# A fourth buffer for the out-state weights beside the output projection, their lag products placed one set later, and one buffer for the normed rows

## The chip, the cores and the metric

One Trainium2 chip (trn2), of which the kernel uses one core. The metric is the device time of one execution in microseconds (us), the median of several runs; lower is better. The engines are TensorE (PE), VectorE (DVE), ScalarE (ACT), GpSimd (POOL) and SyncE (SP, which here only starts transfers).

## The reference

Two layers share one residual stream of D = 1024 features. Layer 0 is windowed attention with grouped heads, layer 1 a bidirectional S5 state space with a gated linear unit. There are 512 latent tokens and 256 context tokens; the branch is 2048 wide.

```python
for i in range(DEPTH):                      # DEPTH = 2: attention, then S5
    h = x * (1.0 + scale) + shift           # the same for the context xc
    pz = h @ w_in                           # branch input and gate path z
    y, yc = attention_mixer(...) or s5_mixer(...)
    x = layer_norm(alpha * x + gate * ((y * silu(z)) @ w_out[i]))
    xc = layer_norm(alpha * xc + gate_c * ((yc * silu(zc)) @ w_out[i]))   # not in the last layer
```

The S5 mixer needs, for each of 128 groups, matrices built from the powers of its complex poles: "out-state" weights, with which a chunk's incoming state acts on its outputs, and lag kernels, with which the inputs act on the outputs of the same chunk. They depend on parameters alone, so the kernel builds them beside layer 0.

## The kernel before

The 768 tokens are six blocks of 128: 0 to 3 latent, 4 and 5 context. Every fp32 product is three products of split operands (`mm3`, L155 to L157): high times high, high times low, low times high. A high part is a copy on ACT, a low part a subtraction on DVE (for the gated heads L145 and L146, for the output weights L582 and L583). Tiles live in pools with a number of buffers each; a scheduler, which works with priorities and a model of the engines, fixes the order of each engine's instructions beforehand, and the pools get fixed addresses, in which a later pool may lie over an earlier one.

**Layer 0's stages.** Attention and its projections (pz, pzc) run to about 666 us; the last steps of a head are the scores, their transposes PT, the split `pth`/`ptl`, the product O, and a store of the gated heads to DRAM (gsc). Then comes the output projection, `outproj0`, to about 843 us: it runs in two halves of 512 columns, each with 8 weights (`wr` raw; `wh` and `woh` high, `wl` and `wol` low), in the first half over the blocks [0,1,2], 3, 4, 5 and in the second over [5,4,0], 1, 2, 3. `gsrc` loads four heads of a block at once (a chunk, 256 KB, from ACT's queue) into one of two raw buffers `gr` and splits them into one of five pairs `gh`/`gl`; each chunk feeds 12 products into `po`. `body` then forms R on DVE (L627, L628), and in the second half the normed rows `nrm` (L633), which PE transposes (h1t, L1021), ACT and DVE turn into the next layer's split input (H1H, H1L), and for latent blocks a store keeps (L636). Behind it layer 1 begins with its input projection: `puc` of context blocks, then `pul` of the latent ones.

**Beside it** the out-state weights are made, 32 sets in all, by `gen_o` (L904): POOL multiplies and adds nine times per set (L924 to L926, then per direction L939, L940, L941 into a tile `gO`), from operands `gcb` and `gpp` that SP loads. ACT fills the tile's edge (L937), SP stores it (osc). Its `lag()` runs 8 small products on PE (L956, 16 rows in the profile), which are evicted into `gK` and stored. `out_q` calls the lag of a set after the next set's `gen_o`. Sets 0 to 19 belong to the attention stage, with four gO buffers; sets 20 to 31 to the pool `go2`, opened in the stage of `outproj0` and served by `side()`, with three. Where a pool has more than three, the first lag product is tied to the last POOL instruction of the next set (L957): the tie is for the scheduler alone, and the engine does not wait for it.

Of the kernel before, what the change touches and what calls it, by code (L numbers as in the profile page):

```python
# [111 lines left out]
F32 = mybir.dt.float32  # L112
# [21 lines left out]
class K:  # L134
# [125 lines left out]
    def ada_gate(self, pool, gpool, l, rows, gscale, gtag):  # L260

        nc, a = self.nc, self.a
        gb = pool.tile([128, 1024], F32, name="gb", tag=gtag, bufs=2)
        nc.sync.dma_start(gb, a["adab"][l, 2048:3072].partition_broadcast(128))
        gates = []
        for r in rows:
            g = gpool.tile([128, 1024], F32, name=f"gate{l}{r}", bufs=1)
            for j in range(2):
                nc.sync.dma_start(g[:, j * 512:(j + 1) * 512], self.gm[64 * l + 32 * j + r].partition_broadcast(128))
            nc.vector.tensor_add(g, g, gb)  # L270
            nc.vector.tensor_scalar(g, g, gscale, None, op0=ALU.mult)
            gates.append(g)
        return gates
# [293 lines left out]
def out_half(k, l, half, groups, gsrc, wpool, body, side=lambda: None):  # L567

    nc, a = k.nc, k.a
    cs = slice(half * 512, half * 512 + 512)  # L570
    W = []
    for c in range(8):
        src = a["wout"][l, c * 256:(c + 1) * 256, cs].rearrange("(e p) n -> p e n", p=128)
        raw = k.wp.tile([128, 2, 512], F32, name="wr", tag="wr", bufs=2)
        if c < 2:
            hi = k.wp.tile([128, 2, 512], F32R, name="wh", tag="wh", bufs=2)
            lo = k.wp.tile([128, 2, 512], F32R, name="wl", tag="wl", bufs=2)
        else:
            hi = wpool[0].tile([128, 2, 512], F32R, name="woh", bufs=6)
            lo = wpool[1].tile([128, 2, 512], F32R, name="wol", bufs=6)  # L580
        nc.sync.dma_start(raw, src)
        nc.scalar.activation(hi, raw, AF.Copy)  # L582
        nc.vector.tensor_sub(lo, raw, f32(hi))  # L583
        W.append((hi, lo))
    for bs in groups:

        n = 256 if half == 1 and bs == groups[-1] else 512
        g = [gsrc(bs[0], e) for e in range(16)] if n < 512 else None
        for c0 in range(0, 512, n):
            po = [k.ps.tile([128, 512], F32, name="po", tag="pj")[:, :n] for b in bs]  # L590
            for e4 in range(0, 16, 4):
                for b, o in zip(bs, po):
                    for e in range(e4, e4 + 4):
                        gh, gl = g[e] if g else gsrc(b, e)
                        wh, wl = (w[:, e % 2, c0:c0 + n] for w in W[e // 2])
                        k.mm3(o, gh, gl, wh, wl, e == 0, e == 15)
            for b, o in zip(bs, po):
                body(b, o, slice(half * 512 + c0, half * 512 + c0 + n))
                side()


def outproj0(k, side):
    tc, nc, a = k.tc, k.nc, k.a
    order = [[[0, 1, 2][:NG]] + [[b] for b in range(NG, 6)], [[5, 4, 0], [1], [2], [3]]]
    R = {}
    g = {}

    def gsrc(b, e):
        if e % 4 == 0:
            ts = slice(b * 128, b * 128 + 128)  # L610
            g[1] = (g.get(1, -1) + 1) % 5
            g[0] = k.load_split(k.gop, "g", [128, 4, 128], k.gsc[e // 4][:, :, ts].rearrange("e p t -> p e t"), 2, 1, nc.scalar, g[1])
        return g[0][0][:, e % 4], g[0][1][:, e % 4]

    def body(half):
        def f(b, po, cs):
            ts = slice(b * 128, b * 128 + 128)
            n = cs.stop - cs.start
            if half == 0:
                r = k.rpool.tile([128, 512], F32, name=f"R{b}")  # L620
            else:
                r = k.op.tile([128, 512], F32, name="R2", bufs=2)
            r = r[:, :n]
            R.setdefault(b, []).append((r, cs))
            xt = k.op.tile([128, 512], F32, name="xt", bufs=2)[:, :n]
            nc.sync.dma_start(xt, a["xtok"][ts, cs])
            nc.vector.tensor_mul(r, po, k.gates0[0 if b < 4 else 1][:, cs])  # L627
            nc.vector.scalar_tensor_tensor(r, xt, ALPHA, r, op0=ALU.mult, op1=ALU.add)  # L628
            if cs.stop == 1024:
                n = k.op.tile([128, 1024], F32, name="nrm", bufs=2)  # L630
                mean, rstd = k.norm(R[b], k.np)
                for x, s in R[b]:
                    nc.vector.tensor_scalar(n[:, s], x, mean, rstd, op0=ALU.subtract, op1=ALU.mult)  # L633
                k.make_h1(b, n)
                if b < 4:
                    nc.sync.dma_start(k.n0[ts], n)  # L636
        return f
    for half in range(2):
        out_half(k, 0, half, order[half], gsrc, k.wop, body(half), side)
# [254 lines left out]
def open_o(k, pool, q0, q1, gob):  # L894

    k.gob, k.dq = gob, q0
    k.dd = pool.tile([128, 16 * (q1 - q0)], F32, name="dd")
    k.nc.sync.dma_start(k.dd, k.a["dd"][:, 16 * q0:16 * q1])
    sg = pool.tile([128, 2], F32, name="sg")
    k.nc.sync.dma_start(sg, k.a["sgn"])  # L900
    k.sg = sg[:, 0:1]
# [96 lines left out]
def prep_h1(k):  # L998

    nc, a = k.nc, k.a  # L1000
    shT, scT = k.sh1
    gc, bc = k.ld("lngc0", [128, 8], a["lngc"][0]), k.ld("lnbc0", [128, 8], a["lnbc"][0])
    G = k.cp.tile([128, 2, 8], F32, name="h1g")
    B = k.cp.tile([128, 2, 8], F32, name="h1b")
    for r in range(2):
        nc.vector.tensor_mul(G[:, r], scT[:, r], gc)
        nc.vector.tensor_mul(B[:, r], scT[:, r], bc)
        nc.vector.tensor_add(B[:, r], B[:, r], shT[:, r])
    k.h1g, k.h1b = G, B


def make_h1(k, b, n):
    nc = k.nc
    r = 0 if b < 4 else 1
    ts = slice(b * 128, b * 128 + 128)
    hf = k.op.tile([128, 8, 128], F32, name="h1f", bufs=1)
    for j in range(2):
        t = k.ps.tile([128, 4, 128], F32, name="h1t", tag="T", bufs=2)
        for i in range(4):
            kk = 4 * j + i  # L1020
            nc.tensor.transpose(t[:, i], n[:, kk * 128:(kk + 1) * 128], k.ident)  # L1021
        for i in range(4):
            kk = 4 * j + i
            g, c = k.h1g[:, r, kk:kk + 1], k.h1b[:, r, kk:kk + 1]
            nc.scalar.activation(hf[:, kk], t[:, i], AF.Identity, bias=c, scale=g)
    H, Lo = k.H1[r]
    ts = slice((b - 4 * r) * 128, (b - 4 * r) * 128 + 128)
    nc.scalar.activation(H[:, :, ts], hf, AF.Copy)
    nc.vector.tensor_sub(Lo[:, :, ts], hf, f32(H[:, :, ts]))
# [310 lines left out]
QA, NB = 20, 5  # L1340
# [7 lines left out]
def main(tc, a):  # L1348
    gw = None
    nq = 0  # L1350
    nc = tc.nc
    k = K(tc, a)
# [4 lines left out]
    def opener(es):  # L1357
        def P(name, bufs=1, **kw):
            if kw.get("space") != DRAM:
                kw["reuse_waits"] = "tile"  # L1360
            return es.enter_context(tc.tile_pool(name=name, bufs=bufs, **kw))
        return P
    with contextlib.ExitStack() as es:
# [106 lines left out]
        with contextlib.ExitStack() as e2:  # L1470
            Q = opener(e2)
            wh = Q("woh")
            k.op = Q("op")
            k.gop = Q("gop")
            k.wop = wh, Q("wol")
            k.rpool = Q("rpool")
            k.make_h1 = lambda b, n: make_h1(k, b, n)
            k.gates0 = k.ada_gate(k.op, k.rpool, 0, (0, 1), 0.5, "nrm")
            prep_h1(k)
            e4 = contextlib.ExitStack()  # L1480
            gw = opener(e4)("go2", side="right")
            open_o(k, gw, QA, 32, 3)
            nb = 0

            def side():
                nonlocal nb
                nb += 1
                if nb <= NB:
                    out_q(QA + (QO - QA) * nb // NB, nb == NB)
                    if nb == NB:  # L1490
                        e4.close()
            outproj0(k, side)
            k.uu = opener(h1c)("uu", side="right")
            first = [uproj_ctx(k, blk) for blk in range(2)]
# [3 lines left out]
        with contextlib.ExitStack() as e2:  # L1498
# [3 lines left out]
            with contextlib.ExitStack() as e3:  # L1502
                R = opener(e3)
                S = []
                with contextlib.ExitStack() as e4:
                    k.up = opener(e4)("up", side="right")
                    e6 = contextlib.ExitStack()
                    gw = opener(e6)("go3")
# [86 lines left out]
```

## Time and profile before

| | |
|---|---|
| time, median of 3 runs | 1488.96 us (1484.08 to 1492.28) |
| the profiled execution: its own time, its span | 1486.36 us, 1484.6 us |
| mean granted clock of PE | 0.983 |
| busy: PE, DVE, ACT, POOL | 1389.9, 1016.6, 667.6, 604.8 us |
| PE waits for a set's gO before lag products, 640 to 850 us | 14.1 us in 8 pieces |

Times inside the span are us from its start. In a timeline a row has the start, the busy time, the engine, the line, the operation, output <- input, how often, and in brackets the idle time before it with what ended it; a queue (ACTq, SPq) shows when a transfer is started. In a row of windows the stretch is followed by its length; then for PE, PEld (PE's weight loads), DVE, ACT and POOL the busy us and, in brackets, the number of instructions; then the granted clock of PE as a share of full speed, the busy share of the DMA engines, and GB/s.

### The profile page before, as it was taken

To read this page: it belongs to the slowest core of one execution; us is meant where nothing else is said; L and a number is where in the kernel's file an instruction comes from. 1 tells how busy PE (TensorE), PEld (TensorE's weight loads), DVE (VectorE), ACT (ScalarE), POOL (GpSimd) and SP (SyncE) were. 2 spreads that over 40 slices of the span, in tenths; PEclk is the share of its full clock that TensorE was granted. 3 is DMA by queue.
4 is the path that set the end of the run, shared out by engine and by line. 5 is a ranking of instruction groups with operands and counts; after the bars stand their busy time and mean duration, and the time that the engine had idled before them with its cause. 6 is when DMAs were issued, how large, how long until landed. Compare 5 with 4: busy or idle time off the path is not lost. (4 is left out here: it accounts for less than half of the span.)

```text
span 1484.6 us, 25841 instructions
## 1 busy us (share of the span) xinstructions
PE 1389.9 (94%) x9092; PEld 1123.2 (76%) x9092; DVE 1016.6 (68%) x2751; ACT 667.6 (45%) x1344; POOL 604.8 (41%) x542
## 2 busy tenths in 40 slices
PE   7999999999986999989878899999999999999997
PEld 2554788898875788877766798888777777888876
DVE  7735748777673677875658813798989986574476
ACT  1310546466463657563333634445556545343220
POOL 0004459999998567973999500000000000000240
PEclk9999999999997999999999999999999999999999
DMA  9876566766674446478697576766767786554541
GB/s 336 284 232 204 161 189 205 230 204 213 190 239 157 132 155 207 148 224 270 200 272 233 178 241 216 223 214 216 239 230 241 242 277 216 182 198 156 185 137 61
DMA packets 252930, 309.60 MB, mean 209 GB/s; under 512 B 45568, under 2 KB 151936, under 8 KB 252800
## 3 DMA queue, kind: packets, MB, share of 16 engines
q1 hardware_dynamic: 227456, 295.36, 62.5%
q10 hardware_dynamic: 25344, 12.59, 2.9%
q8 instruction: 72, 1.18, 0.3%
q14 instruction: 58, 0.48, 0.1%
HBM read 239.20 MB, written 77.07 MB: 213 GB/s over the span
## 5 line engine op out<-in xcount | busy, mean ns | idle before, releaser
L1323 POOL TENSOR_TENSOR xt<-xt,lng 128x512 f32<-128x512 f32 (+1 forms) x9 | 13.3, 1480 | 592.7 <-issue 559.0
L146 DVE TENSOR_TENSOR wl<-wr,wh 128x1024 fp32r<-128x1024 f32 x104 | 142.9, 1374 | 137.7 <-ACT wh L145 135.6
L145 ACT ACTIVATE wh<-wr 128x1024 fp32r<-128x1024 f32 x104 | 109.9, 1058 | 192.7 <-PE pul L156 54.2
L155 PE MATMUL pg<-ga,wh 128*128 128x512 f32 x256 | 100.3, 392 | 0.7 <-ACT ga L1248 0.7
L157 PE MATMUL pg<-ga,wl 128*128 128x512 f32 x256 | 100.5, 393 | 0.0
L887 POOL TENSOR_TENSOR gm<-gB,gE 128x512 f32<-128x512 f32 x56 | 77.7, 1387 | 24.2 <-DVE zs L502 19.9
L941 POOL TENSOR_TENSOR gO<-gO,gX 128x512 f32<-128x512 f32 x58 | 85.2, 1469 | 3.9
L489 DVE TENSOR_TENSOR ptl<-PT,pth 128x512 fp32r<-128x512 f32 (+1 forms) x96 | 60.5, 638 | 36.6 <-ACT pth L488 35.9
L888 POOL TENSOR_TENSOR gm<-gB,gE 128x512 f32<-128x512 f32 x56 | 84.2, 1503 | 0.0
L462 ACT ACTIVATE P<-P,nm 128x512 f32<-128x512 f32 (+1 forms) x64 | 49.6, 775 | 67.2 <-DVE nm L445 66.8
L940 POOL TENSOR_TENSOR gX<-gcb,gpp 128x512 f32<-128x512 f32 x58 | 76.5, 1320 | 3.2
L146 DVE TENSOR_TENSOR gl<-gr,gh 128x512 fp32r<-128x512 f32 x48 | 53.3, 1113 | 33.8 <-ACT gh L145 33.7
L939 POOL TENSOR_TENSOR gO<-gcb,gpp 128x512 f32<-128x512 f32 x58 | 71.5, 1242 | 11.4 <-issue 4.1
L1112 DVE TENSOR_TENSOR x<-m 128x64 f32<-128x64 f32 x376 | 74.5, 217 | 2.4
L155 PE MATMUL O<-pth,vh 128*128 128x256 f32 x176 | 53.4, 303 | 20.4 <-ACT zs L499 12.0
L155 PE MATMUL pq<-hh,wh 128*128 128x512 f32 x160 | 65.9, 413 | 2.8 <-ACT hh L255 2.8
L469 ACT ACTIVATE P<-P,es 128x512 f32<-128x512 f32 (+2 forms) x96 | 61.0, 684 | 15.6 <-DVE es L467 15.3
L156 PE MATMUL pq<-hl,wh 128*128 128x512 f32 x160 | 66.1, 413 | 1.2 <-DVE hl L256 1.2
L488 ACT ACTIVATE pth<-PT 128x512 fp32r<-128x512 f32 (+1 forms) x96 | 52.2, 558 | 31.9 <-PE PT L485 24.9
L485 PE MATMUL PT<-ident,P 128*128 128x128 f32 x352 | 61.6, 277 | 4.4 <-DVE vl L388 3.4
L157 PE MATMUL pq<-hh,wl 128*128 128x512 f32 x160 | 65.1, 407 | 0.3 <-DVE wl L146 0.3
L145 ACT ACTIVATE gh<-gr 128x512 fp32r<-128x512 f32 x48 | 30.2, 630 | 71.5 <-DMA gr<-gsc 44.4
(317 smaller groups left out, 4675.5 us busy)
## 6 DMA issues: line engine op xcount, KB each, us to landing
wr<-w SPq DMA_DIRECT2D x40, 512.0 KB
osc<-gO SPq DMA_DIRECT2D x64, 256.0 KB
wr<-wout SPq DMA_DIRECT2D x32, 512.0 KB
W<-wsc SPq DMA_DIRECT2D x32, 512.0 KB
om<-osc SPq DMA_DIRECT2D x64, 256.0 KB
wr<-glu SPq DMA_DIRECT2D x32, 512.0 KB
gE<-esc SPq DMA_DIRECT2D x56, 256.0 KB
gB<-bt SPq DMA_DIRECT2D x56, 256.0 KB
```

Of the source, the lines that this page charges most:

```text
L145: nc.scalar.activation(hi, raw, AF.Copy)
L146: nc.vector.tensor_sub(lo, raw, f32(hi))
L155: mm(out, wh, mh, start=start, stop=False)
L156: mm(out, wh, ml, start=False, stop=False)
L157: mm(out, wl, mh, start=False, stop=stop)
L485: nc.tensor.transpose(T[:, j, h, :], P[h][:, c * 128:(c + 1) * 128], k.ident)
L887: tt(x(m1), x(B), eb(0), op=ALU.mult)
L888: tt(x(m2), x(B), eb(1), op=ALU.mult)
L939: eng.tensor_tensor(o8, cc(0), pb(0), op=ALU.mult)
L940: eng.tensor_tensor(x8, cc(1), pb(36), op=ALU.mult)
L941: last = eng.tensor_tensor(o8, o8, x8, op=ALU.add)
L1112: nc.vector.tensor_add(x, m[:, :, 0], m[:, :, 1])
```

## The change

The pool `go2` gets a fourth gO buffer (2304 bytes on each partition). With four, the tie of L957 applies to it too, so each lag is placed behind the POOL work of the following set. The normed rows get one buffer instead of two, and so does `gb`, a row of the gate's bias that shares their tag (4096 bytes). The sums done are the same.

```diff
@@ ada_gate
-        gb = pool.tile([128, 1024], F32, name="gb", tag=gtag, bufs=2)
+        gb = pool.tile([128, 1024], F32, name="gb", tag=gtag, bufs=1 if gtag == "nrm" else 2)
@@ outproj0, body
-                n = k.op.tile([128, 1024], F32, name="nrm", bufs=2)
+                n = k.op.tile([128, 1024], F32, name="nrm", bufs=1)
@@ the stage around outproj0
             gw = opener(e4)("go2", side="right")
-            open_o(k, gw, QA, 32, 3)
+            open_o(k, gw, QA, 32, 4)
```

The pools move: the one with `gr` by 4096 bytes, so that the buffer of every second load now lies over the low part hl of the last block of attention's input and over the tables of the rotary positions, where it lay over rotary temporaries.

On PE, before, 193 products of `po` stand ahead of the first lag of `go2`'s sets and 35 to 39 between one and the next in the first 400; the lag of the last set stands within the last block's products of `po`:

```order
L155 MATMUL po<-woh,gh 128x256
L156 MATMUL po<-wol,gh 128x256
L956 MATMUL lag<-gO,gbb 32x128 x8
L1021 MATMUL h1t<-ident,nrm 128x128 x8
L157 MATMUL po<-woh,gl 128x256
```

After, 209 stand ahead of the first and 46 between one and the next; the last two sets' lags stand ahead of the next layer's `pul`:

```order
L155 MATMUL puc<-H1H_8278,wh 128x256
L156 MATMUL puc<-H1L_8279,wh 128x256
L157 MATMUL puc<-H1H_8278,wl 128x256
L1021 MATMUL h1t<-ident,nrm 128x128 x8
L956 MATMUL lag<-gO,gbb 32x128 x16
L155 MATMUL pul<-H1H_8273,wh 128x384
```

The last of the small products moved past the rest of `po` and all 48 of `puc`.

On ACT, before, at the end of the attention (the numbers tell tiles of a name apart: gr_8377, gr_8395 and gr_8413 are the first three loads of the output projection, wh_8327, wh_8333 and woh_8339 its first three weights, pth_8232 and pth_8250 the attention's last):

```order
L144 DMA gr_8377<-gsc0_74 128x4x128
L144 DMA gr_8395<-gsc0_74 128x4x128
L582 ACTIVATE wh_8327<-wr_8326 128x1024
...
L145 ACTIVATE gh_8450<-gr_8449 128x512
L582 ACTIVATE wh_8333<-wr_8332 128x1024
L582 ACTIVATE woh_8339<-wr_8338 128x1024
...
L488 ACTIVATE pth_8232<-PT_8227 128x512
L144 DMA gr_8485<-gsc2_76 128x4x128
L488 ACTIVATE pth_8250<-PT_8245 128x512
```

After:

```order
L582 ACTIVATE wh_8333<-wr_8332 128x1024
L582 ACTIVATE woh_8339<-wr_8338 128x1024
L144 DMA gr_8377<-gsc0_74 128x4x128
L937 ACTIVATE gO_7925<-gcb_7916,sg_4709 128x4x16
L144 DMA gr_8395<-gsc0_74 128x4x128
...
L488 ACTIVATE pth_8232<-PT_8227 128x512
L145 ACTIVATE gh_8378<-gr_8377 128x512
L488 ACTIVATE pth_8250<-PT_8245 128x512
```

The first loads fell back behind the third weight, and the first split of a chunk stands between the last two pth.

On SP, before, the operands of `go2`'s first sets stand behind a load of an output weight (dd and sg are small constants of the pool):

```order
L581 DMA wr<-wout 128x2x512 x2
L966 DMA ksc<-gK 128x240
L581 DMA wr<-wout 128x2x512
L898 DMA dd<-dd 128x192
L900 DMA sg<-sgn 128x2
L910 DMA gcb<-cb 128x512 x2
L912 DMA gpp<-ppsc 128x160 x2
```

After:

```order
L966 DMA ksc<-gK 128x240
L581 DMA wr<-wout 128x2x512
L898 DMA dd<-dd 128x192
L900 DMA sg<-sgn 128x2
L910 DMA gcb<-cb 128x512 x2
L912 DMA gpp<-ppsc 128x160 x2
L581 DMA wr<-wout 128x2x512
```

They moved ahead of one weight load.

## Rows read from the trace of the kernel before

**Rows 1.** Which engines are busy, page section 1 (us, share of the span, instructions):
```profile
PE 1389.9 (94%) x9092; PEld 1123.2 (76%) x9092; DVE 1016.6 (68%) x2751; ACT 667.6 (45%) x1344; POOL 604.8 (41%) x542
```

**Rows 2.** Waits of the stretch 640 to 850 us (us in total, times, longest):
```profile
PE lag L956 <- POOL gO L941: 14.1, 8, 3.5
...
PE lag L956 <- POOL gX L925: 1.8, 1, 1.8
```

**Rows 3.** Busy time of each engine by stretch, 710 to 838 us:
```profile
710.00:785.00 75.00, 62.83 (x337) 49.00 (x337) 46.12 (x51) 25.44 (x52) 72.26 (x60) 0.95 0.84 251
...
785.00:838.00 53.00, 44.73 (x305) 35.49 (x303) 50.14 (x104) 27.90 (x69) 50.13 (x44) 1.00 0.62 187
```

**Rows 4.** Timeline of PE, first and last two of six lags before 785 us:
```profile
717.31 0.65 PE L956 MATMUL lag<-gO,gbb 128*32 128x128 f32 x16 [0.99 <-POOL gO L941]
...
764.00 0.65 PE L956 MATMUL lag<-gO,gbb 128*32 128x128 f32 x16 [2.82 <-POOL gO L941]
...
774.88 0.64 PE L956 MATMUL lag<-gO,gbb 128*32 128x128 f32 x16 [1.84 <-POOL gO L941]
```

**Rows 5.** Timeline of DVE, start and end of the last chain of blocks:
```profile
785.80 0.69 DVE L627 TENSOR_TENSOR R<-po,gate 128x512 f32<-128x512 f32 x1 [0.75 <-PE po L157]
...
848.49 1.19 DVE L633 TENSOR_SCALAR nrm<-R,mv,nt 128x512 f32<-128x512 f32 x3
```

**Rows 6.** Timeline of PE, first product of the next layer:
```profile
851.40 0.44 PE L155 MATMUL pul<-H1H,wh 128*128 128x384 f32 x1 [1.16 <-ACT h1f L1025]
```

**Rows 7.** Timeline of PE, first product of the output projection:
```profile
666.82 0.54 PE L155 MATMUL po<-wh,gh 128*128 128x512 f32 x1
```

**Rows 8.** Windows behind two of those waits, granted clock behind the counts:
```profile
764.70:768.00 3.30, 3.30 (x15) 2.73 (x16) 0.56 (x1) 1.58 (x2) 3.07 (x4) 1.00 0.95 298
...
776.00:780.00 4.00, 4.00 (x12) 3.10 (x11) 1.14 (x3) 0.95 (x3) 3.69 (x4) 0.57 1.13 345
```

**Rows 9.** Tile lag in 480 to 640 us: what its 15 sets waited for:
```profile
  POOL gO L941: 0.7, 2
```

**Rows 10.** Timeline of ACT, around the attention's end and after it:
```profile
650.82 0.39 ACTq L144 DMA_DIRECT2D gr<-gsc  x1
...
656.50 0.63 ACT L145 ACTIVATE gh<-gr 128x512 fp32r<-128x512 f32 x1 [1.99 <-DMA gr<-gsc]
...
659.70 1.07 ACT L488 ACTIVATE pth<-PT 128x512 fp32r<-128x512 f32 x2
...
671.50 0.37 ACTq L144 DMA_DIRECT2D gr<-gsc  x1
...
679.39 0.63 ACT L145 ACTIVATE gh<-gr 128x512 fp32r<-128x512 f32 x1 [3.71 <-DMA gr<-gsc]
...
731.40 0.63 ACT L145 ACTIVATE gh<-gr 128x512 fp32r<-128x512 f32 x1 [3.56 <-DMA gr<-gsc]
```

**Rows 11.** Timeline of POOL, the pool's first and last instruction:
```profile
704.62 0.40 POOL L924 TENSOR_TENSOR gX<-gcb,gpp 128x128 f32<-128x128 f32 x1 [22.43 <-DMA gpp<-ppsc]
...
836.66 1.27 POOL L941 TENSOR_TENSOR gO<-gO,gX 128x512 f32<-128x512 f32 x1
```

**Rows 12.** Timeline of DVE, splits of two output weights:
```profile
692.17 1.23 DVE L583 TENSOR_TENSOR wol<-wr,woh 128x1024 fp32r<-128x1024 f32 x1 [2.79 <-ACT woh L582]
...
695.42 1.23 DVE L583 TENSOR_TENSOR wol<-wr,woh 128x1024 fp32r<-128x1024 f32 x1 [1.14 <-ACT woh L582]
```

**Rows 13.** Timeline of DVE, normed rows of blocks 0 and 1:
```profile
819.00 1.38 DVE L633 TENSOR_SCALAR nrm<-R,mv,nt 128x512 f32<-128x512 f32 x2
...
826.11 2.84 DVE L633 TENSOR_SCALAR nrm<-R,mv,nt 128x512 f32<-128x512 f32 x2
```

**Rows 14.** Windows over single sets of POOL, busy time of each engine:
```profile
750.75:764.00 13.25, 10.43 (x51) 8.00 (x51) 11.20 (x12) 5.35 (x10) 12.87 (x9) 0.87 0.83 265
...
774.90:783.44 8.54, 8.54 (x44) 6.76 (x45) 3.19 (x5) 2.55 (x7) 8.15 (x8) 0.80 1.11 349
...
828.72:837.98 9.26, 7.71 (x75) 7.31 (x75) 8.91 (x19) 5.76 (x14) 8.87 (x8) 1.00 0.43 142
```

## The prediction

> **What bounds the kernel now.** I read the busy shares first, then the waits of the stretch that the change touches, then the stretch by engine, and last the single instructions. TensorE (PE) is busy for 94% of the span [rows 1]; so a change can shorten the time by what PE waits for, by what it runs at the lower clock, or not at all. Beside the output projection PE sat idle for 14.1 us, in 8 pieces, before a set's lag products until GpSimd (POOL) had written the set's last gO, and once for 1.8 us until the small operands were there [rows 2]. In 710 to 785 us POOL is busy for 72.3 of 75 us while PE is not full [rows 3]: POOL sets the pace, PE queues behind each set, since PE's order is static and a lag product that waits holds every product behind it. Six of the waits lie before 785 us; the timeline of PE has the first at 717.31 (0.99 us), the last but one at 764.00 (2.82) and the last at 774.88 (1.84), and the six come to 12.2 us [rows 4].
>
> From 785.8 us on VectorE (DVE) takes over: 50.1 us busy of 53 [rows 3], one chain of R, norm and normed rows from block 5 at 785.80 to block 3 at 848.49 [rows 5]. Only then can the next layer's first full product (pul) start, at 851.40 [rows 6]. Waits of PE after 785 us are hidden behind that chain; so are 2.0 us of the 14.1, by the six above. The time counts where pul starts; behind it I see nothing that the change alters, so what pul gains the kernel gains.
>
> **The change part by part.**
>
> *Lag products one set later, with a fourth gO.* The same work is done: the same POOL, ACT and DVE instructions, and the 16 rows of each lag. What changes is where the lags stand on PE. Before, the first lag of this pool (set 20) stands behind 193 of the po products, then one lag per about 36; after, behind 209, then one per 46. Up to the end of block 5 in the second half (408 products) PE then passes five of these sets, no longer six.
>
> PE needs 118.2 us from its first po at 666.82 [rows 7] to that end, 785.05 (the R at 785.80 less the 0.75 us for which DVE waited for it [rows 5]). Taken off: the six waits, 12.2; one lag of 0.64 us [rows 4], which passes behind that end; and two stretches of half clock. After two of the waits the granted clock was 0.57 for 4 us (752 to 756, and 776 to 780, which is shown), a mean of its two levels, 2.4 and 1.2 GHz; that loses 0.43 of 4 us, 1.7 us each time. After the wait that ended at 764.00 it stayed at 1.00 [rows 8]. Sum: 12.2 + 0.6 + 3.4 = 16.2 us. Does POOL allow that? Set 24, the last that PE now passes in this stretch, was written when its lag began at 764.00 [rows 4], and the lag and some 15 products (0.23 us each, by 118.2 less the waits, the clock and the lags over 408) follow: 764.0 + 0.6 + 3.5 = 768.1, a gain of up to 16.9. So a removed wait isn't met again one set later. That the rule works in this kernel the attention stage shows: there four buffers and the same order are in use already, and 15 sets cost PE 0.7 us [rows 9], against 14.1 here.
>
> *What the fourth buffer displaces.* The tile is paid for with a second buffer of the normed rows, and the pools behind shift. The even buffer of the gated heads' loads (gr) now lies over the last block of the attention's input (hl) and over the rotary tables; it used to lie over rotary temporaries that are free early. So these loads cannot start until the attention's projections are through. In ACT's order the first gr issue falls back behind the third weight's woh, and one of the last two pth stands behind the first gh. On the old times ACT issued the loads long before that, had five chunks split when po began, and the last two pth ran at 659.70 [rows 10]. Now the first load goes out at about 659. It lands in 5.7 us (650.82 to 656.50) to 7.9 us (671.50 to 679.39) [rows 10], so at 665 to 667, and the last pth follows it, 4 to 6 us later than before. ACT gains something back, since its waits for landings ahead of that pth go away, such as 1.99 us at 656.50 [rows 10]. Call the delay of po 1 to 5 us. After that the feed has no head start: two loads in flight, so a pair per 5.7 to 7.9 us, 2.9 to 4.0 per chunk, where PE takes one per 12 products, 2.8 us. For the first 12 chunks that adds nothing to some 5 us, part of it inside the first delay. I put both together at 1 to 8 us and take 4.5, the middle, since both ends rest on landings that the trace has. Path of PE and DVE: 16.2 - 4.5 = 11.7 us.
>
> *POOL's own end.* From 704.62, after 22.4 us of waiting for its operands, POOL works through 12 sets almost without a gap and ends at 836.66 + 1.27 = 837.9 [rows 11], 11.1 us per set. The changed order puts the last two lags straight ahead of pul, behind all po and puc. So pul can't start before 837.9 + 0.64 = 838.6, against 851.40 [rows 6]: at most 12.8 us, unless POOL begins earlier. It may: its loads (gcb, gpp) pass one weight load on the SP queue, which waits until a raw weight is split; the two splits are 3.25 us apart (692.17 and 695.42 [rows 12]). That gives 0 to 3.25 us. I take 0, because the splits themselves sit behind the late gh on ACT.
>
> *One buffer for normed rows (and gb).* Each block's nrm now waits for the transposes of the block before and, for the latent blocks, for its store. The tightest pair is block 0, written at 819.00 + 1.38, and block 1 at 826.11 [rows 13]: 5.7 us apart, against a landing of 5.7 to 7.9 [rows 10]: 0 to 2.2 us. The other latent pairs lie farther apart. The transposes follow their rows at once. I take 0, with 2.2 as upper bound; without the cover of DVE's other work it would be paid in full, since DVE is the chain there. gb is used once, before the stage: nothing.
>
> The later of the two paths decides: 11.7 of 12.8. The profiled execution took 1486.36 us, 2.6 below the median of 1488.96, so on its own scale this is 1474.7; on the median's, 1477.3, and I say **1477**.
>
> **The rivals.**
>
> *POOL begins earlier and the feed holds.* If gcb passes its weight load (3.25) and the feed costs 1, both paths give 15 to 16 us: 1473. For it: the SP order. Against: ACT's late loads.
>
> *The feed eats most.* With a delay of 9 to 16 us the gain is 0 to 7: about 1485. For it: the landing of 7.9 us, in a stretch in which ACT waited again and again for such loads. Against: the 19 chunks after the first five were split between 666.82 and 731.40 [rows 7, 10], 3.4 us each, with all those waits of PE in the stretch.
>
> *POOL slows down.* DVE's work is pressed into a shorter stretch, and sets get longer where DVE is busy: 13.25 us with DVE busy 11.20 of them (85%), 8.54 with 3.19 (37%) [rows 14]. That is about 1 us per 10 points. A stretch shorter by 12 us raises DVE's share from 75% to 83%; 0.8 us more on 12 sets is 9.6 us, and the gain 3: 1486. Against: the last set, 9.26 us with DVE busy 8.91 [rows 14], so the share alone does not set it. The Trainium skill (SBUF — State Buffer, "SBUF: two separate sides") says that GpSimd and a DVE instruction with two SBUF inputs take one port pair as an exclusive lock, so that a fourth buffer would make POOL no faster and a denser DVE would make it slower. By that rule this rival would be the forecast, at 1486; the trace agrees with it at 750 to 783 us and not in the last set.
>
> *The feed never catches up (slower).* If every pair of loads takes 7.9 us from 665 on, the last of the 24 chunks lands at 665 + 11 x 7.9 = 752, where ACT split it at 731.40 before [rows 10]: 20.5 us late. Waits for data would drop the clock as those for gO did, so only 12.8 come off: +7.7, 1496.7. It decides from 12.8 us of delay on. Against: 3.4 us per chunk, as above, is less than 7.9 per pair.
>
> *It does nothing.* If POOL's sets come as late against PE's new places as against the old, PE still waits: a set takes 11.1 us, and 46 products with a lag some 11.3. The head start (16 products, 3.7 us) is all that is won, and the delay at the start takes that: 1488. Against: the attention stage [rows 9].
>
> **How the numbers follow.** Forecast (8 to 13.5 us faster) 0.43; deeper 0.14; feed eats most 0.15; POOL slows 0.10; nothing 0.06; slower 0.12, nrm's waits with it. About 0.5% (7.4 us) is what a measurement of this kernel tells from no change. Faster by more than that: forecast, deeper, and a little of the edges, 0.60; within: 0.28; slower: 0.12. The range leaves out the slower case and the far end of the deeper one: 1470 to 1488. The likeliest case alone has 1475.5 to 1481.
>
> **What would show it.** Right: no wait of PE for gO above 1 us between 700 and 785; clock 1.00 there; R of block 5 at about 774 and pul at about 840; the two last lags directly before pul, waiting for POOL or just not; first po at 668 to 672. Wrong, and how: PE idle at po products with ACT's gh or its loads as releaser and a low clock in 667 to 700 (the feed); sets of POOL above 12 us (POOL); DVE idle before nrm until a store has landed (the single buffer); a po that starts after 675 (the attention's end).

## The result, and the profile after

The changed kernel takes 1499.22 us (median of 4 runs, 1498.01 to 1500.85) against 1490.26 of the kernel before on the same chip: a ratio of 1.0072, 95% interval 1.0050 to 1.0093. By the medians it is slower by 9.0 us, by the ratio by some 11; 12 us faster were forecast. The profiled execution took 1498.52 us, with a span of 1496.7 and a mean granted clock of 0.975 (0.983 before).

The two spans differ by 12.1 us. Of these 9.2 lie ahead of pul: 5.1 at the R of block 5, and 4.2 between the last normed rows and pul; the chain between the two took 62.7 us before and 62.6 after. The other 2.9 lie behind pul, and tell nothing: there the traces of this case, one execution each, differ by up to 9.6 us (630.1 to 639.7).

What the change was to remove is gone. PE's waits in 662 to 865 us no longer name POOL at all; before they named it for 14.1 and 1.8 us [rows 2]. Others stand in their place:

```profile
PE h1t L1021 <- DVE nrm L633: 8.7, 5, 3.0
PE po L155 <- DVE R L627: 7.1, 2, 3.8
PE po L155 <- ACT gh L145: 3.1, 3, 2.5
PE po L157 <- DVE gl L146: 2.3, 4, 0.8
PE po L156 <- DVE wl L583: 2.3, 1, 2.3
PE lag L956 <- DVE gK L965: 1.4, 1, 1.4
```

The timeline of PE of the changed kernel has where that leads. The first po started 3.9 us earlier than before [rows 7], but the next layer's pul 9.2 us later [rows 6]:

```profile
662.91 0.63 PE L155 MATMUL po<-wh,gh 128*128 128x512 f32 x1
...
750.80 0.64 PE L956 MATMUL lag<-gO,gbb 128*32 128x128 f32 x16
757.43 0.77 PE L155 MATMUL po<-wh,gh 128*128 128x512 f32 x1 [3.27 <-DVE R L627]
...
782.08 0.39 PE L157 MATMUL po<-woh,gl 128*128 128x512 f32 x1
...
791.75 0.76 PE L155 MATMUL po<-wh,gh 128*128 128x512 f32 x1 [3.85 <-DVE R L627]
...
857.13 1.08 PE L956 MATMUL lag<-gO,gbb 128*32 128x128 f32 x16
859.61 1.08 PE L956 MATMUL lag<-gO,gbb 128*32 128x128 f32 x16 [1.40 <-DVE gK L965]
860.62 0.69 PE L155 MATMUL pul<-H1H,wh 128*128 128x384 f32 x1
```

The row at 782.08 is the last product for block 5 in the second half (the 408th of po). Before, it stood 3.3 us later:

```profile
785.37 0.39 PE L157 MATMUL po<-woh,gl 128*128 128x512 f32 x1
```

DVE's timeline shows why R, which PE now waits for, is late all the same. The sum of block 5 was done by 782.5, those of the other two blocks of the group by 787.9 (791.75, where PE went on, less its wait of 3.85), yet the R of block 5 ran at 790.92, 8.4 us after its sum. Before, it followed its sum at once [rows 5]. The two traces have another order on DVE: before, 36 of the 48 chunks are split ahead of this R, after, 38. The two further ones, at 787.16 and 790.31, belong to the next block, and they waited for ACT, and so for their loads. The last block's normed rows, the end of the chain, came at 853.50, against 848.49:

```profile
787.16 0.69 DVE L146 TENSOR_TENSOR gl<-gr,gh 128x512 fp32r<-128x512 f32 x1 [3.62 <-ACT gh L145]
...
790.31 0.69 DVE L146 TENSOR_TENSOR gl<-gr,gh 128x512 fp32r<-128x512 f32 x1 [0.86 <-ACT gh L145]
790.92 0.68 DVE L627 TENSOR_TENSOR R<-po,gate 128x512 f32<-128x512 f32 x1
...
853.50 2.96 DVE L633 TENSOR_SCALAR nrm<-R,mv,nt 128x512 f32<-128x512 f32 x3
```

Before, the 36th split is the last ahead of R (785.80), and the 37th stands behind it:

```profile
783.47 1.58 DVE L146 TENSOR_TENSOR gl<-gr,gh 128x512 fp32r<-128x512 f32 x1 [1.14 <-ACT gh L145]
...
788.26 1.80 DVE L146 TENSOR_TENSOR gl<-gr,gh 128x512 fp32r<-128x512 f32 x1 [1.04 <-ACT gh L145]
```

On ACT the loads can be seen: the third chunk, for which ACT waited 6.34 us at the start, and the 37th, for which it waited 4.29 us just ahead of that R:

```profile
667.72 0.63 ACT L145 ACTIVATE gh<-gr 128x512 fp32r<-128x512 f32 x1 [6.34 <-DMA gr<-gsc]
...
786.50 0.63 ACT L145 ACTIVATE gh<-gr 128x512 fp32r<-128x512 f32 x1 [4.29 <-DMA gr<-gsc]
```

Before, ACT waited nearly as long for the 37th chunk and had it later:

```profile
787.60 0.63 ACT L145 ACTIVATE gh<-gr 128x512 fp32r<-128x512 f32 x1 [3.92 <-DMA gr<-gsc]
```

So at this place no load had become later; R had come to stand behind it. The feed was late in the first half: its last chunk, the 24th, began its split on ACT at 738.23, against 731.40 before [rows 10].

POOL, which ran almost without a gap before [rows 11], waits now. In both waits shown a set's first write to gO starts where a lag has just ended: 751.39 is the end of the lag that began at 750.80 (0.64 us), whatever releaser the row names. It began 6.8 us earlier than before, but its last instruction ends at 856.3, no longer at 837.9:

```profile
697.84 0.40 POOL L924 TENSOR_TENSOR gX<-gcb,gpp 128x128 f32<-128x128 f32 x1 [16.90 <-DMA gpp<-ppsc]
...
724.20 1.07 POOL L939 TENSOR_TENSOR gO<-gcb,gpp 128x512 f32<-128x512 f32 x1 [4.00 <-PE lag L956]
...
751.39 1.06 POOL L939 TENSOR_TENSOR gO<-gcb,gpp 128x512 f32<-128x512 f32 x1 [4.92 <-issue]
...
855.03 1.27 POOL L941 TENSOR_TENSOR gO<-gO,gX 128x512 f32<-128x512 f32 x1
```

And the granted clock fell more often. These four windows of 10 us each have a wait of PE for chunks, a weight or R; before, the clock was 0.83 twice in 700 to 800 us, after two waits for gO:

```profile
690.00:700.00 10.00, 7.54 (x27) 5.32 (x26) 3.65 (x4) 2.84 (x6) 2.16 (x4) 0.83 0.93 305
740.00:750.00 10.00, 7.74 (x28) 5.93 (x27) 8.24 (x10) 4.57 (x9) 6.23 (x5) 0.83 0.51 148
750.00:760.00 10.00, 6.73 (x37) 4.87 (x36) 8.10 (x7) 4.55 (x6) 8.45 (x6) 0.84 0.93 290
790.00:800.00 10.00, 8.25 (x37) 6.00 (x38) 7.15 (x12) 2.17 (x4) 5.05 (x6) 0.66 0.94 281
```

Over the whole stage the difference lies behind block 5's last product. First the kernel before, from its first po to that product's end and on to pul:

```profile
666.82:785.76 118.94, 104.96 (x541) 82.38 (x537) 71.35 (x81) 40.03 (x79) 89.13 (x76) 0.96 0.83 255
785.76:851.40 65.64, 56.10 (x409) 46.51 (x407) 61.07 (x129) 35.87 (x89) 49.45 (x42) 1.00 0.62 186
```

Then the changed kernel:

```profile
662.91:782.47 119.56, 108.53 (x538) 81.75 (x538) 75.68 (x81) 40.03 (x75) 81.13 (x70) 0.95 0.77 236
782.47:860.62 78.15, 62.02 (x425) 50.46 (x424) 64.92 (x133) 37.72 (x94) 56.53 (x49) 0.90 0.63 197
```

### The profile page after: what moved, and what is told of

The parts are those of the page before. It is cut to its first block, busy times and chain, and to the rows that moved or that the text cites. A ratio compares the mean times of both kernels' runs of the same rounds, so it can differ in the third digit from the quotient of the medians.

```text
span 1496.7 us, 25845 instructions
## 1 busy us (share of the span) xinstructions
PE 1401.4 (94%) x9092; PEld 1129.8 (75%) x9092; DVE 1020.7 (68%) x2751; ACT 667.5 (45%) x1344; POOL 602.9 (40%) x542
## 5 line engine op out<-in xcount | busy, mean ns | idle before, releaser
L939 POOL TENSOR_TENSOR gO<-gcb,gpp 128x512 f32<-128x512 f32 x58 | 68.1, 1180 | 32.7 <-issue 18.2
L155 PE MATMUL po<-woh,gh 128*128 128x512 f32 (+1 forms) x156 | 60.4, 387 | 2.6 <-ACT gh L145 2.6
```

What stands on the lines that cost most here:

```text
L155: mm(out, wh, mh, start=start, stop=False)
L939: eng.tensor_tensor(o8, cc(0), pb(0), op=ALU.mult)
```

## Experiments

Eighteen kernels ran, each beside the kernel before. "R" is the start of the R of block 5 in the second half, "sum" the start of PE's last product for it, "tail" the time from the last normed rows (their start) to pul; these three are from one profiled execution each, which need not stand for the median (e9's took the least time of its twelve, e7's and e16's the most of theirs). "Clock" is the mean granted clock over all runs of a kernel. By the changed kernel's four runs and the others' 5 to 12, differences in the ratio below about 0.002 tell nothing.

| kernel | median us | ratio to before, 95% | sum | R | tail | clock |
|---|---|---|---|---|---|---|
| before | 1487.1 to 1490.3 | 1 | 785.37 | 785.80 | 2.9 | 0.980 to 0.981 |
| changed | 1499.22 | 1.0072 (1.0050 to 1.0093) | 782.08 | 790.92 | 7.1 | 0.977 |
| e1 single rows alone | 1494.20 | 1.0035 (1.0020 to 1.0049) | 788.44 | 790.66 | 2.9 | 0.981 |
| e2 changed, no tie | 1495.17 | 1.0050 (1.0031 to 1.0068) | 789.57 | 794.05 | 2.9 | 0.980 |
| e3 changed, raw buffers back | 1494.58 | 1.0037 (1.0021 to 1.0052) | 773.78 | 783.32 | 10.1 | 0.977 |
| e4 changed, last sets untied | 1495.39 | 1.0052 (1.0036 to 1.0068) | 785.29 | 792.59 | 5.4 | 0.978 |
| e5 e3, tie to mid-set | 1494.30 | 1.0043 (1.0025 to 1.0061) | 781.93 | 786.40 | 2.9 | 0.978 |
| e6 changed, tie to mid-set | 1493.00 | 1.0033 (1.0017 to 1.0049) | 789.61 | 791.14 | 2.9 | 0.980 |
| e7 e3, no tie | 1491.89 | 1.0021 (1.0005 to 1.0038) | 785.79 | 786.22 | 2.9 | 0.980 |
| e8 e1, raw buffers back | 1488.47 | 1.0008 (0.9990 to 1.0026) | 784.51 | 785.70 | 2.9 | 0.981 |
| e9 before, rearrangement later | 1494.97 | 1.0049 (1.0029 to 1.0068) | 782.01 | 782.45 | 2.9 | 0.979 |
| e10 before, free lags | 1492.07 | 1.0032 (1.0014 to 1.0049) | 787.79 | 789.10 | 2.9 | 0.980 |
| e11 e9 and e10 | 1493.22 | 1.0040 (1.0023 to 1.0057) | 788.97 | 791.34 | 2.9 | 0.980 |
| e12 e3, rearrangement later | 1493.75 | 1.0042 (1.0024 to 1.0060) | 778.77 | 789.06 | 10.0 | 0.976 |
| e13 before, half loads | 1488.60 | 1.0002 (0.9982 to 1.0021) | 784.84 | 788.75 | 2.9 | 0.980 |
| e14 e10, half loads | 1491.78 | 1.0025 (1.0010 to 1.0039) | 790.80 | 796.95 | 2.9 | 0.979 |
| e15 changed, half loads | 1488.67 | 0.9996 (0.9980 to 1.0012) | 777.45 | 785.68 | 7.4 | 0.978 |
| e16 e3, half loads | 1489.99 | 1.0006 (0.9986 to 1.0026) | 777.47 | 786.69 | 7.4 | 0.978 |
| e17 e3, spare banks | 1492.09 | 1.0027 (1.0006 to 1.0049) | 776.90 | 787.24 | 10.0 | 0.978 |
| e18 e17, last sets untied | 1493.02 | 1.0026 (1.0010 to 1.0042) | 777.57 | 788.25 | 5.6 | 0.977 |

**The parts of the change, e1 to e4.** The theories were the late feed (A), the tail (B) and the single buffer itself (C). e1 is the two `bufs=1` edits alone, on the kernel before.

> The single buffer for the normed rows and gb alone, with three gO buffers and no tie: the gated heads' loads lie over the attention's input as after the change. Theory A (the feed: the loads lost their head start, and PE's early gains go into waits for chunks): about as slow as the changed kernel or slower, ratio to before 1.004 to 1.012, with the waits for gO still there in part and PE waiting for gh and gl between 670 and 700. Theory B (the tail: two lags straight ahead of pul, and the normed rows later): the lags stand before pul's block again, so within 0.3% of before. Theory C (the single buffer itself makes DVE wait): slower by 0.3 to 0.8%, with the last nrm late although the feed is fine.

e2 leaves the tie to the attention's sets:

```diff
-                if g == 0 and d == 1 and after is not None and k.gob > 3:
+                if g == 0 and d == 1 and after is not None and k.gob > 3 and k.dq == 0:
```

> The changed kernel without the tie for the twelve sets beside the output projection: four gO buffers, lags at about 36 products' distance again, the last lag ahead of po's end. Theory A (feed): still slow, ratio to before 1.004 to 1.010. Theory B (tail): pul no longer waits for two lags, 4 us come back, ratio 1.002 to 1.005. If the tie was what removed PE's waits for gO, they are back (5 to 14 us in the stretch).

e3 puts the fifth pair of split chunks (4096 bytes) into a pool ahead of the raw buffers, which so come to lie where they lay before:

```diff
+            k.gop4 = Q("gop4")
             k.gop = Q("gop")
...
-2, 1, nc.scalar, g[1])
+2, 1, nc.scalar, g[1], k.gop4 if g[1] == 4 else None)
```

> The changed kernel with the fifth pair of split chunks in a pool of its own ahead of the raw buffers, so that these lie where they did before and the first loads may start during the attention: the order of ACT around the attention's end is that of the kernel before. Theory A (feed): the early loss of about 6 us by 700 is gone and most of the forecast gain appears: ratio to before 0.992 to 1.000. Theory B (tail): the two last lags still stand ahead of pul; ratio 1.004 to 1.008.

e4 ties sets up to 28 only (`and q < 29`).

> The changed kernel with the tie for sets up to 28 only: one lag, no longer two, stands straight ahead of pul. Theory B (tail): 1 to 2.5 us less than the changed kernel (the second lag waited 1.4 us for the eviction of the first and took 1.1): ratio to before 1.0055 to 1.0065. Theory A (feed): no change beyond that, the stretch to 845 us as in the changed kernel.

The addresses cost: e1, which has them and the single buffers, is slower by 0.35%, and e3, which differs from the changed kernel in them (and in the orders that follow), gives back about half of the 0.72%. In e3 po ended 10 us earlier than in the changed kernel and R came at 783.32, and yet the time stayed above before: R came 9.2 us after its sum was done, the tail took 10.1 us, and in the list of e3's waits PE stands longest for DVE:

```profile
PE po L156 <- DVE R L628: 10.0, 2, 5.5
PE h1t L1022 <- DVE nrm L634: 7.8, 6, 4.0
PE lag L957 <- DVE gK L966: 3.3, 1, 3.3
```

e4's 0.2% agrees with (B), but lies within what the runs tell apart; e2 did not bring the lag waits back in full (10.8 us) and was slow all the same.

**POOL paced by lags, e5 to e8.** e5 and e6 tie a lag to the add of the next set's first direction, in e3 and in the changed kernel:

```diff
-        last = eng.tensor_tensor(o8, o8, x8, op=ALU.add)
+        add = eng.tensor_tensor(o8, o8, x8, op=ALU.add)
+        last = last if d and k.dq else add
```

> The kernel with the raw buffers back where they were, and the tie moved from the last POOL instruction of the next set to the add of that set's first direction: a lag is placed half a set behind its own set, no longer a whole one. Theory D (lockstep: with four buffers a set takes two, so POOL's set after next waits for a lag that the tie has put behind the next one; PE paces POOL and POOL ends late): POOL's waits for lags are gone, POOL ends near 838 us, no lag stands right ahead of pul, pul at 843 to 847, ratio to before 0.993 to 0.998. If only the feed matters: as with the raw buffers back and the whole tie, ratio 1.002 to 1.005. If the single row buffer matters: no better than 1.000.

> The changed kernel with the tie moved to the add of the next set's first direction; the loads stay over the attention's input. Theory A plus D: the lockstep goes, the late feed stays: ratio to before 1.001 to 1.005, that is 3 to 8 us below the changed kernel. Theory A alone: 1.006 to 1.008.

e7 is e2 and e8 is e1, both with the raw buffers back.

> Four gO buffers, no tie for these sets, the raw buffers back where they were, one row buffer. PE's order of lags is nearly that of before. If the fourth buffer without the tie gains nothing: PE's waits for gO are back at 9 to 14 us, ratio 0.998 to 1.002. If the fourth buffer by itself is what removes waits: waits below 4 us, ratio 0.992 to 0.996.

> Three gO buffers, no tie, one buffer for the normed rows and gb, the raw buffers back: of the change only the single buffer is left, and PE's order is that of before but for a few products. Theory A says the single buffer costs nothing: ratio 0.998 to 1.002. Theory C (DVE waits for transposes and stores): 1.002 to 1.006, with nrm waiting.

e8 settles two points. The single row buffer costs nothing that can be told (1.0008), and moving the raw buffers costs about 0.27% by itself (e1 against e8), little more than the runs tell apart. At the old addresses the fourth buffer with its tie costs 0.29% (e3 against e8); without the tie it gains nothing (e7, 1.0021, with PE's waits for gO at 11.6 us). PE's waits for gO are 13.7 us in e8, as before. e5 did to POOL what the theory said: in its list of POOL's waits only the first loads are left, and POOL ended at 835.9, the tail was 2.9.

```profile
POOL gX L925 <- DMA gpp<-ppsc: 21.8, 1, 21.8
```

But e5 was no faster (1.0043 where 0.993 to 0.998 was expected): R came at 786.40, as before, and the chain from there to the last normed rows (855.13) took 68.7 us, where before took 62.7. So the lockstep of POOL and PE is real, and at the old addresses it is not the price. With the late loads it may be part of it: e6 lies 0.39% below the changed kernel, in intervals that just don't touch, with the same R and a tail of 2.9 in place of 7.1 us.

**Is there anything to gain? e9 to e12.** e9, e11 and e12 start the rearrangement of sets 16 to 23 after set 28. In e10 and e11 the lags of `go2` read a row of the gate instead of `gO` and `gbb`, so that their values are left out and nothing of POOL's can hold them.

```diff
-        if q % 8 == 7:
+        if q % 8 == 7 and q != 23:
             gen_m0(k, q // 8)
+        if q == 28:
+            gen_m0(k, 2)
```

> The kernel before with one thing moved: the rearrangement of sets 16 to 23 (m0sc, eight transfers), started after set 28 and no longer after set 23, out of the stretch in which the second half's weights and the chunks of its first three blocks are loaded. Theory E (transfers bound PE around the change of halves, whatever the lags do): block 5's R a few us before 785 us, but the waits for gO then cap it; ratio 0.994 to 1.000. If transfers don't bound: 0.999 to 1.002.

> The kernel before with the lag products of these twelve sets reading a row of the gate in place of POOL's results (their values are left out, the rest is as before): PE can't wait for POOL at all. If the 14 us of waits were PE's to gain: R of block 5 at 770 to 775, ratio 0.989 to 0.994. Theory E (they covered transfers that are late anyway, and then the chain on DVE): R of block 5 not before 781, ratio 0.997 to 1.002, new waits of PE for chunks, weights or DVE's R of 6 us or more in the stretch to 785.

> The free lags and the later rearrangement together (the lags' values are left out). Theory E: with fewer transfers around the change of halves PE gets ahead, R of block 5 at 772 to 779, ratio 0.991 to 0.997, clearly below the free lags alone. If neither transfers nor waits bound: ratio as for the free lags alone.

> The raw buffers back, four gO buffers and the whole tie as in the change, and the rearrangement later. Theory E: R of block 5 at 776 to 781 (783.3 without), ratio 0.998 to 1.002, the tail with two lags ahead of pul still in it. Otherwise as without: 1.003 to 1.005.

e10 takes away all the waits that the forecast's first term counts. With no wait for POOL possible, R came at 789.10, 3.3 us later than before, and the kernel was slower by 0.32%, outside both ranges given. But more than the waits has changed in it: with nothing to hold the lags, the scheduler put nine of the twelve ahead of block 5's last product, where before has six and the changed kernel five. PE waits for a lag's PSUM bank, of which there is one, until DVE has evicted the lag before, and DVE's evictions stand in order behind splits that wait for chunks:

```profile
PE h1t L1021 <- DVE nrm L633: 8.3, 3, 6.8
PE lag L956 <- DVE gK L965: 7.7, 6, 2.9
```

So e10 shows that the removed waits need not pay; it does not price the change's own order of lags.

Theory E in its narrow form fell: the rearrangement is not what holds PE. e9 took 0.49% longer (in its one trace, where po began 6.2 us earlier than before, R came 3.4 us earlier), and e11 and e12 differ from e10 and e3 by less than can be told.

**Are the loads the cause? e13 to e16.** Two of a chunk's four heads are loaded and split twice, so two heads of each are left out of the values, and the splits keep their size:

```diff
+        if name == "g":
+            q.dma_start(raw[:, 0:2], src[:, 0:2])
+            two = raw[:, 0:2][:, None].to_broadcast([128, 2, 2, 128])
```

> The kernel before with half the bytes in each chunk load: two of the four heads are loaded and split twice, so that all work but the transfer stays (two heads of each chunk are left out of the values). Theory F (without the waits for gO, PE is bound by chunks and weights that arrive late, and by what stands behind their splits on DVE and ACT in order): the waits for gO stay at 10 to 15 us and hide the gain; ratio to before 0.995 to 1.000. Rival G (the chain on DVE from block 5 on, and the tail, bound whatever arrives): 0.998 to 1.001.

> The free lags (values left out) with half the bytes in each chunk load. Theory F: now PE can use the waits that are gone: R of block 5 at 772 to 778, ratio 0.988 to 0.995, at least 4 us below the half loads alone. Rival G: within 2 us of the half loads alone.

> The changed kernel with half the bytes in each chunk load. Theory F: the feed no longer costs what the change laid on it: R of block 5 at 774 to 782, but two lags stay ahead of pul and POOL is still paced by PE's lags: ratio 0.996 to 1.002, 6 us or more below the changed kernel. Rival G: 1.003 to 1.007.

> Raw buffers back, four gO buffers, whole tie, and half the bytes in each chunk load. Theory F: R of block 5 at 772 to 780, ratio 0.993 to 1.000. Rival G: as with whole loads, 1.002 to 1.005.

Halving the bytes takes the changed kernel from 1.0072 to 0.9996, with intervals that lie apart, and does nothing for the kernel before (1.0002). So most of what the change lost hangs on the bytes of the chunk loads, though the tail of 7.4 us is still there in e15; e16 is level too (1.0006), by an interval that overlaps e3's. It doesn't make the removed waits pay: e14 is at 1.0025, with R at 796.95, and its lags, ten of them ahead of block 5's last product, waited longer for the eviction:

```profile
PE lag L963 <- DVE gK L972: 13.2, 6, 3.6
```

That is rival G's result for the gain, and theory F's for the loss. The scheduler knows the smaller size, so the orders in e15 differ from the changed kernel's (the first lag of `go2` stands behind 215 products of po, not 209); what the bytes do and what the order does can't be told apart here.

**What eats the gain? e17 and e18.** e17 gives the groups of one block the two PSUM banks of the attention's scores, with PE's order as in e3, and e18 ties sets up to 26 only.

```diff
-name="po", tag="pj")[:, :n] for b in bs]
+name="po", tag="pj" if l or len(bs) > 1 else "S", bufs=None if l or len(bs) > 1 else 2)[:, :n] for b in bs]
```

> The raw buffers back, four gO buffers, the whole tie (as e3), and the sums po of the groups of one block in the two PSUM banks that the attention's scores have left, so that PE need not wait for DVE's R of the group before. PE's order is that of e3 instruction for instruction. If the 10.0 us for which PE waited for R in e3 were a price of their own: they are gone, POOL, which PE's lags pace, ends 3 us or more earlier, and the ratio is 0.997 to 1.002 (e3: 1.0037). Rival G (DVE's chain and the tail bind whatever PE gains): within 0.15% of e3.

> As e17, with the tie for sets up to 26 only, so that one lag and not two stands ahead of pul and the last sets' lags come earlier. Theory B (tail): the time from the last normed rows to pul falls from 10 us (e3) to 3 to 5, the ratio to 0.993 to 0.999; this would beat both kernels. If POOL's last set still ends late: no better than e17.

In e17 PE was through with block 5's sum 8.5 us earlier than before, and R still came 1.4 us later than before, behind 38 splits, on DVE:

```profile
776.90 0.40 PE L158 MATMUL po<-woh,gl 128*128 128x512 f32 x1
...
787.24 0.68 DVE L628 TENSOR_TENSOR R<-po,gate 128x512 f32<-128x512 f32 x1
```

The 10.0 us for which PE waited for R are gone, and the waits of PE came back at the normed rows and at gO:

```profile
PE h1t L1022 <- DVE nrm L634: 12.7, 5, 7.6
PE lag L957 <- POOL gO L942: 4.0, 1, 4.0
PE po L158 <- DVE gl L147: 3.5, 3, 2.0
```

e17 lies 0.1% below e3, which is within what can be told; POOL, which was held for 7.1 us by ACT (it fills the tile's edge, in its own order), ended at 854.8. e18's tail fell to 5.6 and its time did not. No version beat the kernel before.

## Why the prediction was wrong

**The step that failed** is "Path of PE and DVE: 16.2 - 4.5 = 11.7 us": that what PE saves reaches the R of block 5. The waits for gO did go, and POOL was early enough, as worked out. But in the changed kernel PE did not get faster, and in other kernels that ran, where it did, R did not follow.

*On PE.* From its first po to its last product for block 5 PE took 119.2 us, against 118.5 before. The waits in that stretch came to 11.0 us under other names (R 3.3, gh 3.1, gl 2.3, wl 2.3) where before had 14.0 (gO 12.2, wol 1.8), and the clock was no better (0.95 and 0.96). PE was 3.3 us ahead there only because po had begun 3.9 us earlier.

*On DVE.* In the kernels that tie these lags to the next set's last instruction and have the feed earlier or smaller (e3, e12, e15 to e18) PE took 107.7 to 113.1 us for that stretch, so 5 to 11 of the 16.2 us were there. R came 7.8 to 10.3 us after its sum all the same. In each of these kernels, and in the changed one, DVE's order has 38 splits ahead of this R, where before has 36, and one of the added two waited on ACT for its load, for 2.4 to 4.3 us. Of the others e4, e13 and e14 have 38 too, and R 3.5 to 6.9 us after its sum; in those with 36 it is 0 to 4.1 us. So DVE's order and the loads set R, and not PE.

[rows 5] had the sign of it, and I misread it twice. DVE's wait of 0.75 us ended when PE's sum was done, so PE's end is 785.8 and not 785.05, and PE needed 118.9 us. And DVE had been free for no more than those 0.75 us, since a split that had waited for ACT: with DVE's order and its splits as they were, an earlier PE could bring R forward by 0.75 us, not by 11.7.

**The delay by the loads** (1 to 8 us, 4.5 taken) was right in its cause and wrong in its place. The attention did not end later: the first load went out at 653.45 and not at 659, its data was split at 659.01, the last pth followed at 659.55, and po began 3.9 us earlier (over all the traces it begins between 660.6 and 669.9). What was missing was the head start: two chunks were split when po began, where before five were. e1 against e8 gives 4 us for it with the old lag order (0.27% of 1488), e3 against the changed kernel 5 us (0.35%), both inside the 1 to 8 us. With half the bytes (e15) the kernel is level with before. The rival "the feed eats most" had this mechanism with the gain still under it, "the feed never catches up" with the right side and 1496.7. That this is close to what was measured is luck: it needs the 24th chunk 20.5 us late, and it was 6.8 late (738.23 against 731.40).

**POOL's own end** was taken as 837.9 whatever PE does. That was wrong too: with two tiles per set, a fourth buffer lets POOL be one set ahead, and a lag placed behind the next set's work holds the set after that. POOL waited for lags instead of PE for POOL and ended at 856.3. So the two lags ahead of pul, foreseen in their place, made the tail 7.1 us, 4.2 more than before.

**The clock** was to gain 3.4 us. It lost instead, above all behind block 5's last product: 0.90 of full speed on to pul, where before had 1.00. This is not of one execution. Over all runs the mean clock is 0.976 to 0.978 in every kernel with that tie, 0.979 to 0.981 in those without a tie for these sets, and 0.978 and 0.980 with the tie to mid-set. A difference of 0.003 over 1490 us is 4 to 5 us of PE's time (an estimate), of the size of what the fourth buffer and its tie cost; but e15 and e16 have the low clock too and are level with before, so what it costs stays open.

**The single row buffer** was rightly costed at nothing (e8). **POOL slower under a denser DVE** was not put to the test: e5, without waits for lags, has POOL's sets in 129.5 us (133.3 before), but DVE was no denser beside them (busy for 77% of that time, 76% before). The rule of the Trainium skill (SBUF — State Buffer, "SBUF: two separate sides"), that GpSimd and a DVE instruction with two SBUF inputs lock one port pair against each other, spoke for longer sets; no run here shows whether a denser DVE makes them longer.

**What stays open.** By the runs the parts come to 0.27% for the addresses (e1 against e8), 0.29% for the fourth buffer with its tie (e3 against e8) and 0.08% for e8 itself, 0.64 of the 0.72%; the first two are little above what can be told. No kernel put the R of block 5 ahead of the splits of later chunks, so that DVE's order eats the gain is read from the traces and not shown by a run. Of the eighteen kernels only e8, e13, e15 and e16 are level with before, and e9, in which only eight transfers are moved (and the scheduler's orders with them), is slower by 0.49%. In e5, e10 and e14 the raw buffers lie where they lay before, the tail is 2.9 us, and still 0.25 to 0.43% are lost, in part after R (chains of 59 to 69 us on DVE, from one execution each). Which of DVE's waits in order make up that rest was not taken apart.

## What to carry to other kernels

A wait that is seen on the busiest engine is worth its length only if what that engine feeds, and what feeds it, could have been earlier: look at what stands ahead of the consumer in its own engine's order, and how long that engine had been free. A kernel that skips the wait's cause (e10) is worth running, but its order has to be compared too. When a buffer is bought with memory, look up what the later pools now lie over: the first loads of a stage may lose a head start that nothing in the code names. And an extra buffer that is spent on placing the consumer one step later leaves the producer as tightly coupled as it was.

## What the runs showed of the hardware

PE's waits between the first po and pul did not go away with their cause; they came back under other names (23.4 us before, 27.0 after, 22.7 in e10, and 20 to 28 in all twenty traces). And the releaser that a row names can be wrong: POOL's "issue" of 4.92 us at 751.39 ends with a lag on PE to within 0.1 us.
